# Rotary embedding on one core: four batches to a tile, the first tile in one piece, and tables of 32 partitions spread by TensorE

## The chip, the cores and the metric

The kernel runs on one core of a Trainium2 chip. The metric is the device time in microseconds (us), the median of several executions. A separate profiled execution leaves a trace; its span runs from the first instruction to the end of the last transfer, and all places in time ("at 92 us") count from its start.

## What is computed

`x` holds 16 batches of 512 rows of 1024 floats; a row is 16 heads of 64 values, and each head is split into two halves of 32. `cos` and `sin` have one row of 32 values for each of the 512 positions. In and out are 33.5 MB each, all in 32-bit floats.

```
x1, x2 = x[..., :half_dim], x[..., half_dim:]          # x as (16, 512, 16 heads, 64)
cos, sin = cos[None, :, None, :], sin[None, :, None, :]
out = concatenate([x1 * cos - x2 * sin, x1 * sin + x2 * cos], axis=-1)
```

## The kernel before, in words

**Rows and tiles.** A *row* in the kernel (index `u`, 0 to 63) is one row of x on each of 128 partitions: 128 rows of 4 KB, 0.5 MB in all. Rows come in tiles that are loaded by one DMA and stored by one DMA. The first two and last two tiles (L40) are one batch each, 4 rows, 2 MB, 16 KB in a piece per partition. The six between are two batches each, 8 rows, 4 MB, 32 KB per partition, with the two batches on alternate partitions (L108 to L111). In a tile of one batch, a partition holds 4 neighbouring positions, in a tile of two batches 8, so the two kinds need tables laid out differently.

**The ring.** `x_sb` holds 40 of the 64 rows. The loads of rows 0 to 39 are issued at once on ACT's queue, the tables' two loads right behind the first (L167 to L175). The loads of rows 40 to 63 reuse places: ACT issues them in the middle of its work, after rows 17, 25 and 33, and each waits first until the store of the rows that lay there before has landed (L193 to L196). The wait after row 33 is for the store of rows 16 to 23, and two loads follow it.

**One row.** There are two products and a sum. DVE multiplies the row by cos into PSUM (`mul`, L302; three such buffers). POOL multiplies the row with its halves swapped by a table of -sin and +sin into `t2_sb` (L263; eight buffers), mostly two rows in an instruction. In a tile of 8, row 3's swapped product is DVE's (`V2`, L295). The sum is DVE's (`comb`, L313, written over the row in `x_sb`) or, for rows 1, 3 and 5 of eight (`PE2`, L51, not in the first and last four rows), TensorE's: it adds the product to the PSUM buffer with a matmul by the identity (L225), and ACT copies the result to `x_sb` (L192). DVE's product for row u waits until the buffer of row u - 3 is free, so it can wait for ACT's copy.

**Stores.** SP issues the store of a tile once its last row is summed (L162).

**Tables.** cos and sin are loaded as 128 partitions of 4 positions (512 B each). The first tile's tables come straight from there: DVE copies cos (L273), ACT makes -sin and +sin (L183, L184). The tables for tiles of two batches are spread by TensorE: ACT makes `pick` from an identity (L178), two matmuls (L209) put positions of two partitions side by side in PSUM, and ACT makes -sin and +sin again (L187, L188). DVE copies the row it needs for row 3 (L280, L281). POOL waits for the first table at row 0 and the second at row 8 (L252 to L255).

Of the kernel before, what the change touches and what calls it, by code (L numbers as in the profile page):

```python
# [6 lines left out]
def bass_split_heads_rope_kernel(  # L7
# [16 lines left out]
    batch, seq, dim = x.shape  # L24
    H = int(num_heads)
# [4 lines left out]
    R2 = 2 * R1  # L30
    assert R1 * P == seq and R1 == 4 and batch % 2 == 0

# [6 lines left out]

    singles = (0, 1, batch - 2, batch - 1)  # L40
    tiles = [(b, R1 if b in singles else R2) for b in range(batch) if b in singles or b % 2 == 0]
    NT = len(tiles)
    RING = 5 * R2

    rows = [(t, r) for t, (_, n) in enumerate(tiles) for r in range(n)]
    NU = len(rows)
    EARLY = (NU - RING) // R2


    V_ROW = 3  # L50
    PE2 = [R1 <= u < NU - R1 and u % R2 in (1, 3, 5) for u in range(NU)]  # L51
    V2 = [tiles[t][1] == R2 and r == V_ROW for t, r in rows]

# [18 lines left out]
    with ExitStack() as stack:  # L72
        x_sb = stack.enter_context(nc.sbuf_tensor([P, RING, H, 2, HALF], fp32))
        t2_sb = stack.enter_context(nc.sbuf_tensor([P, NT2, H, 2, HALF], fp32))
        stage = stack.enter_context(nc.sbuf_tensor([P, 2, R1 * HALF], fp32))
        s1_sb = stack.enter_context(nc.sbuf_tensor([P, R1, 2, HALF], fp32))
        s2_sb = stack.enter_context(nc.sbuf_tensor([P, R2, 2, HALF], fp32))
        ident = stack.enter_context(nc.sbuf_tensor([P, P], fp32))
        pick = stack.enter_context(nc.sbuf_tensor([P, 2, P // 2, 2], fp32))
        zero = stack.enter_context(nc.sbuf_tensor([P, BANK], bf16))  # L80
        tab_ps = stack.enter_context(nc.psum_tensor([P, BANK], fp32))
        pair_ps = stack.enter_context(nc.psum_tensor([P, 2, 2, R1, HALF], fp32))
        t1_ps = stack.enter_context(nc.psum_tensor([P, NT1, H * HD], fp32))
# [17 lines left out]

        c1_ps = tab_ps[:, 0:R1 * HALF].rearrange("p (r d) -> p r d", d=HALF)
        v_ps = tab_ps[:, R1 * HALF:R1 * HALF + HD].rearrange("p (t d) -> p t d", d=HALF)

        def c_of(t, r):
            return c1_ps[:, r, :] if tiles[t][1] == R1 else pair_ps[:, r // R1, 0, r % R1, :]

        x1 = x.rearrange("b (s r) d -> b s (r d)", r=R1)  # L108
        o1 = out.rearrange("b (s r) h d -> b s (r h d)", r=R1)
        x2 = x.rearrange("b (s r) d -> s b (r d)", r=R2)  # L110
        o2 = out.rearrange("b (s r) h d -> s b (r h d)", r=R2)  # L111
        xs = x_sb[:].rearrange("p n h t d -> p n (h t d)")

        def in_dram(single, pairs, t):
            b, n = tiles[t]
            return single[b] if n == R1 else pairs[:, b:b + 2, :]

        def in_sbuf(t):
            b, n = tiles[t]
            k = b * R1 % RING  # L120
            return x_sb[:, k:k + n].rearrange("p n h t d -> p (n h t d)")
# [5 lines left out]
        def swapped(k):  # L127
            return x_sb[:, k, :, ::-1, :]
# [20 lines left out]
        def stores_of(k):  # L149

            return sum(b * R1 // R2 == k for b, _ in tiles)

        def load(eng, t):
            eng.dma_start(in_sbuf(t), in_dram(x1, x2, t)).then_inc(sem_in[t], 16)  # L154

        def on_sync(sp):
            for u in range(NU):
                t, r, k = where(u)
                if r == tiles[t][1] - 1:
                    wait_added(sp, u)  # L160
                    k = u // R2
                    sp.dma_start(in_dram(o1, o2, t), in_sbuf(t)).then_inc(sem_out[k] if k < EARLY else sem_rest, 16)  # L162
            sp.wait_ge(sem_rest, 16 * sum(stores_of(k) for k in range(EARLY, NU // R2)))

        def on_scalar(ae):
            later = {}
            for t, (b, n) in enumerate(tiles):  # L167
                if b * R1 + n <= RING:
                    load(ae, t)
                else:  # L170

                    later.setdefault((b * R1 - RING) // R2 * R2 + R2 - 1 + LAG, []).append(t)
# [5 lines left out]
            ae.activation(  # L178
                pick[:], ident[:].rearrange("q (s k) -> q k s", k=2)[:, :, :, None].broadcast_to([P, 2, P // 2, 2]), COPY
            ).then_inc(sem_g, 1)  # L180
            ae.wait_ge(sem_sin, 16)
            sv = stage[:, 1, :].rearrange("s (r d) -> s r d", d=HALF)
            ae.activation(s1_sb[:, :, 0, :], sv, COPY, scale=-1.0)  # L183
            ae.activation(s1_sb[:, :, 1, :], sv, COPY).then_inc(sem_s, 1)  # L184
            ae.wait_ge(sem_t, 2)
            s2 = s2_sb[:].rearrange("p (k r) t d -> p k r t d", r=R1)
            ae.activation(s2[:, :, :, 0, :], pair_ps[:, :, 1, :, :], COPY, scale=-1.0)  # L187
            ae.activation(s2[:, :, :, 1, :], pair_ps[:, :, 1, :, :], COPY).then_inc(sem_s, 1)  # L188
            for u in range(NU):
                if PE2[u]:  # L190
                    ae.wait_ge(sem_e, n_pe[u])
                    ae.activation(xs[:, u % RING, :], t1_ps[:, u % NT1, :], COPY).then_inc(sem_a, 1)  # L192
                for t in later.get(u, ()):  # L193
                    k = (tiles[t][0] * R1 - RING) // R2
                    ae.wait_ge(sem_out[k], 16 * stores_of(k))
                    load(ae, t)  # L196

        def on_tensor(pe):
# [6 lines left out]
            pe.wait_ge(sem_g, 1)  # L205
            pe.wait_ge(sem_cos, 16)
            pe.wait_ge(sem_sin, 16)
            for k in range(2):
                pe.matmul(  # L209
                    pair_ps[:, k].rearrange("p c r d -> p (c r d)"),  # L210
                    pick[:, k].rearrange("q s b -> q (s b)"),
                    stage[:].rearrange("q c f -> q (c f)"),
                    start=True,
                    stop=True,
                ).then_inc(sem_t, 1)
# [19 lines left out]
        def on_gpsimd(pl):  # L235
# [11 lines left out]
            for u in range(NU):  # L247
                if V2[u] or (G2[u] and u % 2 == 1):
                    continue
                t, r, k = where(u)  # L250
                n = 2 if G2[u] else 1
                if (t, r) == (0, 0):  # L252
                    pl.wait_ge(sem_s, 1)
                if (t, r) == (2, 0):
                    pl.wait_ge(sem_s, 2)  # L255
                if r == 0:
                    pl.wait_ge(sem_in[t], 16)
                if n == 2 and u + 1 >= NT2:
# [3 lines left out]
                table = (s1_sb if tiles[t][1] == R1 else s2_sb)[:, r:r + n]  # L262
                pl.tensor_tensor(  # L263
                    t2_sb[:, u % NT2:u % NT2 + n],
                    x_sb[:, k:k + n, :, ::-1, :],
                    table[:, :, None, :, :].broadcast_to([P, n, H, 2, HALF]),
                    mult,
                ).then_inc(sem_p, 1)

        def on_vector(ve):  # L270
            ve.memset(zero[:], 0.0).then_inc(sem_z, 1)  # L271
            ve.wait_ge(sem_cos, 16)
            ve.tensor_copy(c1_ps, stage[:, 0, :].rearrange("s (r d) -> s r d", d=HALF)).then_inc(sem_c, 1)  # L273
            ve.wait_ge(sem_c, 1)
            ve.wait_ge(sem_w, NT1 * EH)

            def pair_tables():
                ve.wait_ge(sem_s, 2)
                row = pair_ps[:, V_ROW // R1, 1, V_ROW % R1, :]
                ve.tensor_scalar_mul(v_ps[:, 0, :], row, -1.0).then_inc(sem_c, 1)  # L280
                ve.tensor_copy(v_ps[:, 1, :], row).then_inc(sem_c, 1)  # L281

            first_v = V2.index(True)

            def mul(u):
                t, r, k = where(u)
                if r == 0:
                    ve.wait_ge(sem_in[t], 16)
                if (t, r) == (2, 0):
                    pair_tables()  # L290
                if u == first_v:
                    ve.wait_ge(sem_c, 3)
                if V2[u]:
                    wait_t2_free(ve, u)
                    ve.tensor_tensor(t2_sb[:, u % NT2, :, :, :], swapped(k), over_heads(v_ps), mult)  # L295
                if u >= NT1:
# [7 lines left out]
                    x_sb[:, k, :, :, :].rearrange("p h t d -> p (h t) d"),  # L304
                    c_of(t, r)[:, None, :].broadcast_to([P, 2 * H, HALF]),
                    mult,
# [57 lines left out]
```

## Time and profile before

| | us |
|---|---|
| runs: median (lowest to highest) | 161.18 (161.13 to 161.49) |
| the profiled execution: span | 159.6 |
| what a run's time has around that span (median less span) | 1.6 |
| busy: DVE / POOL / PE / ACT | 129.6 / 131.7 / 64.4 / 24.3 |
| one POOL product of two rows (x23) / of one row (x12) | 4.53 / 2.36 |
| one DVE product / sum | 1.22 / 1.22 |
| one ACT copy of a row | 1.02 |
| moved by DMA | 67.25 MB, 421 GB/s over the span |
| first load lands / last load lands / last store issued | 8.5 / 140.25 / 151.9 |

An operation's own time includes a little overlap with the next: in a row of DVE operations one starts every 1.13 us, in a row of POOL products every 4.5 us (two rows) or 2.28 us (one row). The trace has for each DMA its issue, its size and the time to its landing; the queue q10 is ACT's (loads), q1 SP's (stores).

### The profile page before, as it was taken

To read this page: it belongs to the slowest core of one execution; us is meant where nothing else is said; L and a number is where in the kernel's file an instruction comes from. 1 tells how busy PE (TensorE), PEld (TensorE's weight loads), DVE (VectorE), ACT (ScalarE), POOL (GpSimd) and SP (SyncE) were. 2 spreads that over 40 slices of the span, in tenths; PEclk is the share of its full clock that TensorE was granted. 3 is DMA by queue.
4 is the path that set the end of the run, shared out by engine and by line. 5 is a ranking of instruction groups with operands and counts; after the bars stand their busy time and mean duration, and the time that the engine had idled before them with its cause. 6 is when DMAs were issued, how large, how long until landed. Compare 5 with 4: busy or idle time off the path is not lost.

```text
span 159.6 us, 499 instructions
## 1 busy us (share of the span) xinstructions
PE 64.4 (40%) x94; PEld 22.2 (14%) x94; DVE 129.6 (81%) x117; ACT 24.3 (15%) x27; POOL 131.7 (82%) x41
## 2 busy tenths in 40 slices
PE   6050017076408870789067400575058506900000
PEld 1020011021102220222021100211021102300000
DVE  0069947999999989998999629999999999556900
ACT  0420002004300250023102040023202310220000
POOL 1069999999999999999999798992999999089400
PEclk9999999759985589557759985589957995585555
DMA  5999999999999999999999999999999999999997
GB/s 144 396 466 472 394 411 431 448 476 402 394 448 406 495 419 402 476 435 402 443 435 435 394 476 435 402 460 394 427 456 448 443 394 423 472 419 435 386 456 300
DMA packets 3169, 67.25 MB, mean 421 GB/s; under 512 B 352, under 2 KB 608, under 8 KB 608
## 3 DMA queue, kind: packets, MB, share of 16 engines
q10 hardware_dynamic: 1728, 33.69, 49.8%
q1 hardware_dynamic: 1440, 33.56, 48.9%
q14 instruction: 1, 0.01, 0.0%
HBM read 33.69 MB, written 33.55 MB: 421 GB/s over the span
## 4 chain that ended last, share of the span: by engine, by line
DMA 61%; DVE 17%; POOL 5%; PE 5%; issue 4%; ACTq 1%; ACT 1%; DVEq 0%; POOLq 0%; SPq 0%
DMA x_sb<-in_x_dram 43%; DMA out_dram<-x_sb 18%; DVE t_ps L302 8%; DVE x_sb L313 7%; POOL t_sb L263 5%; PE t_ps L225 5%; DVE t_sb L295 2%; ACT x_sb L192 1%; ACTq L154 1%; ACTq L175 1%; DVE tab_ps L280 0%; DVEq L312 0%; DVE tab_ps L281 0%; DVEq L299 0%; POOLq L259 0%
## 5 line engine op out<-in xcount | busy, mean ns | idle before, releaser
L263 POOL TENSOR_TENSOR t_sb<-x_sb,s_sb 128x2048 f32<-128x2048 f32 (+1 forms) x35 | 131.0, 3784 | 17.1 <-DMA x_sb<-in_x_dram 8.3
L225 PE MATMUL t_ps<-t_sb,ident 128*128 128x512 f32 x84 | 59.6, 857 | 69.1 <-DVE t_ps L302 56.7
L302 DVE TENSOR_TENSOR t_ps<-x_sb,pair_ps 128x1024 f32<-128x1024 f32 x48 | 57.5, 1221 | 5.2 <-ACT x_sb L192 5.2
L313 DVE TENSOR_TENSOR x_sb<-t_ps,t_sb 128x1024 f32<-128x1024 f32 x43 | 52.2, 1216 | 5.9 <-POOL t_sb L263 5.9
L192 ACT ACTIVATE x_sb<-t_ps 128x1024 f32<-128x1024 f32 x21 | 21.4, 1024 | 107.6 <-PE t_ps L225 99.9
L225 PEld LDWEIGHTS t_ps<-t_sb,ident 128*128 128x128 f32 x84 | 20.3, 267 | 108.2 <-DVE t_ps L302 78.7
L302 DVE TENSOR_TENSOR t_ps<-x_sb,tab_ps 128x1024 f32<-128x1024 f32 x16 | 19.2, 1222 | 2.6 <-DMA x_sb<-in_x_dram 2.5
L295 DVE TENSOR_TENSOR t_sb<-x_sb,tab_ps 128x1024 f32<-128x1024 f32 x6 | 7.3, 1209 | 0.0
L273 DVE COPY tab_ps<-stage 128x128 f32<-128x128 f32 x1 | 0.3, 296 | 7.6 <-DMA stage<-in_cos_dram 7.6
L209 PE MATMUL pair_ps<-stage,pick 128*128 128x256 f32 x4 | 2.0, 667 | 5.1 <-DMA stage<-in_sin_dram 5.1
L202 PE MATMUL t_ps<-zero 128*128 128x512 bf16 x6 | 2.7, 629 | 1.3 <-DVE zero L271 1.3
L178 ACT ACT_TABLE_LOAD x1 | 1.3, 1283 | 5.5 <-issue 5.5
L209 PEld LDWEIGHTS pair_ps<-stage,pick 128*128 128x128 f32 x4 | 1.2, 324 | 6.1 <-issue 6.0
L202 PEld LDWEIGHTS t_ps<-zero 128*128 128x128 bf16 x6 | 0.7, 136 | 2.4 <-DVE zero L271 1.2
L271 DVE MEMSET zero<- 128x256 uint32 x1 | 0.3, 272 | 0.9 <-PEq L346 0.9
L187 ACT ACTIVATE s_sb<-pair_ps 128x256 f32<-128x256 f32 x1 | 0.4, 384 | 1.7 <-PE pair_ps L209 1.7
L183 ACT ACTIVATE s_sb<-stage 128x128 f32<-128x128 f32 x1 | 0.3, 310 | 1.8 <-DMA stage<-in_sin_dram 1.8
L236 POOL MEMSET ident<- 128x128 f32 x1 | 0.2, 205 | 0.3 <-POOLq L346 0.3
L178 ACT ACTIVATE pick<-ident 128x256 f32<-128x256 f32 x1 | 0.4, 416 | 0.0
L188 ACT ACTIVATE s_sb<-pair_ps 128x256 f32<-128x256 f32 x1 | 0.4, 377 | 0.0
L238 POOL TENSOR_SCALAR_AFFINE_SELECT ident<-ident 128x128 f32<-128x128 f32 x1 | 0.3, 295 | 0.1
L346 POOL MEMSET const-float32-0.0<- 128x1 f32 x1 | 0.1, 99 | 0.3 <-issue 0.3
(6 smaller groups left out, 1.0 us busy)
## 6 DMA issues: line engine op xcount, KB each, us to landing
x_sb<-in_x_dram ACTq DMA_DIRECT2D x6, 4096.0 KB, 38.7
out_dram<-x_sb SPq DMA_DIRECT2D x6, 4096.0 KB, 25.3
x_sb<-in_x_dram ACTq DMA_DIRECT2D x4, 2048.0 KB, 22.7
out_dram<-x_sb SPq DMA_DIRECT2D x4, 2048.0 KB, 16.1
stage<-in_cos_dram ACTq DMA_DIRECT2D x1, 64.0 KB, 7.5
stage<-in_sin_dram ACTq DMA_DIRECT2D x1, 64.0 KB, 7.2
```

The lines of the kernel that those rows point to most:

```text
L154: eng.dma_start(in_sbuf(t), in_dram(x1, x2, t)).then_inc(sem_in[t], 16)
L175: ae.dma_start(stage[:, i, :], table.rearrange("(s r) d -> s (r d)", r=R1)).then_inc(sem, 16)
L178: ae.activation(pick[:], ident[:].rearrange("q (s k) -> q k s", k=2)[:, :, :, None].broadcast_to([P, 2, P // 2, 2]), COPY).then_inc(sem_g, 1)
L187: ae.activation(s2[:, :, :, 0, :], pair_ps[:, :, 1, :, :], COPY, scale=-1.0)
L192: ae.activation(xs[:, u % RING, :], t1_ps[:, u % NT1, :], COPY).then_inc(sem_a, 1)
L202: pe.matmul(t1_ps[:, k, b * BANK:(b + 1) * BANK], zero[:, 0:P], zero[:], start=True, stop=True).then_inc(sem_w, 1)
L209: pe.matmul(pair_ps[:, k].rearrange("p c r d -> p (c r d)"), pick[:, k].rearrange("q s b -> q (s b)"), stage[:].rearrange("q c f -> q (c f)"),
L225: ins = pe.matmul(t1_ps[:, u % NT1, b * BANK:(b + 1) * BANK], ident[:], t2[:, b * BANK:(b + 1) * BANK], start=False, stop=True, skip_group ...
L263: pl.tensor_tensor(t2_sb[:, u % NT2:u % NT2 + n], x_sb[:, k:k + n, :, ::-1, :], table[:, :, None, :, :].broadcast_to([P, n, H, 2, HALF]), ...
L295: ve.tensor_tensor(t2_sb[:, u % NT2, :, :, :], swapped(k), over_heads(v_ps), mult)
L302: ve.tensor_tensor(t1_ps[:, u % NT1, :].rearrange("p (h d) -> p h d", d=HALF), x_sb[:, k, :, :, :].rearrange("p h t d -> p (h t) d"), c_of ...
L313: ve.tensor_tensor(xs[:, k, :], t1_ps[:, u % NT1, :], t2_sb[:, u % NT2, :, :, :].rearrange("p h t d -> p (h t d)"), add,).then_inc(sem_v, 1)
```

## The change

A tile now comes from a run of four batches (2048 rows): a partition holds 16 neighbouring positions of one batch, and 32 partitions make a batch. Each run of 16 rows is two tiles of 8 rows, the lower and the upper half of each partition's positions; only the very last tile stays cut in two of 4. So there are seven tiles of 4 MB and two of 2 MB. The pieces of a 4 MB tile are 32 KB each, 64 KB apart. The first tile is 4 MB, loaded and stored whole. All tiles share one layout of the tables: 16 positions on each of 32 partitions, loaded as 32 partitions of 2 KB, spread to all four batches by one matmul each for cos and sin (`pick` is an identity of 32, repeated four times). ACT makes -sin and +sin from the second matmul's result; DVE reads cos directly from PSUM, and for rows 3 and 11 makes -sin in the place next to sin. The direct tables for the first tile go. Five loads are issued up front instead of six.

```diff
+    R4 = 4 * R1
...
-    singles = (0, 1, batch - 2, batch - 1)
-    tiles = [(b, R1 if b in singles else R2) for b in range(batch) if b in singles or b % 2 == 0]
+    runs = batch // 4
+    tiles = []
+    for c in range(runs):
+        for r0 in range(0, R4, R2):
+            if (c, r0) == (runs - 1, R4 - R2):
+                tiles += [(c, r0, R1), (c, r0 + R1, R1)]
+            else:
+                tiles.append((c, r0, R2))
...
-    V_ROW = 3
+    V_ROWS = (3, 11)
     PE2 = [R1 <= u < NU - R1 and u % R2 in (1, 3, 5) for u in range(NU)]
-    V2 = [tiles[t][1] == R2 and r == V_ROW for t, r in rows]
+    V2 = [tiles[t][2] == R2 and r == V_ROWS[0] for t, r in rows]
...
+        xr = x.rearrange("(c b) (s r) d -> c (b s) r d", b=4, r=R4)
+        outr = out.rearrange("(c b) (s r) h d -> c (b s) r (h d)", b=4, r=R4)
...
+        def in_dram(view, t):
+            c, r0, n = tiles[t]
+            return view[c][:, r0:r0 + n, :].rearrange("p r d -> p (r d)")
...
-                        ae.dma_start(stage[:, i, :], table.rearrange("(s r) d -> s (r d)", r=R1)).then_inc(sem, 16)
+                        ae.dma_start(stage[:, i, :], table.rearrange("(s r) d -> s (r d)", r=R4)).then_inc(sem, 16)
...
+            ae.activation(pick[:], ident[0:P // 4, None, 0:P // 4].broadcast_to([P // 4, 4, P // 4]), COPY).then_inc(sem_g, 1)
             ae.wait_ge(sem_t, 2)
...
+            ae.activation(s_sb[:, :, 0, :], sin_ps, COPY, scale=-1.0)
+            ae.activation(s_sb[:, :, 1, :], sin_ps, COPY).then_inc(sem_s, 1)
...
+            for i, (table_ps, sem) in enumerate(((cos_ps, sem_cos), (sin_ps, sem_sin))):
+                pe.wait_ge(sem, 16)
                 pe.matmul(
+                    table_ps.rearrange("p r d -> p (r d)"),
+                    pick[:].rearrange("q b s -> q (b s)"),
+                    stage[:, i, :],
...
-                if (t, r) == (0, 0):
+                if u == 0:
                     pl.wait_ge(sem_s, 1)
-                if (t, r) == (2, 0):
-                    pl.wait_ge(sem_s, 2)
...
-            ve.wait_ge(sem_cos, 16)
-            ve.tensor_copy(c1_ps, stage[:, 0, :].rearrange("s (r d) -> s r d", d=HALF)).then_inc(sem_c, 1)
-            ve.wait_ge(sem_c, 1)
             ve.wait_ge(sem_w, NT1 * EH)
+            ve.wait_ge(sem_t, 1)
+
+            def v_table():
+                ve.wait_ge(sem_s, 1)
+                for r in V_ROWS:
+                    ve.tensor_scalar_mul(sin_ps[:, r - 1, :], sin_ps[:, r, :], -1.0).then_inc(sem_c, 1)
...
-                if (t, r) == (2, 0):
-                    pair_tables()
+                if u == first_v - 1:
+                    v_table()
```

More of the change, by code (lines that the diff above doesn't have):

```diff
@@ L30, in bass_split_heads_rope_kernel @@
     R2 = 2 * R1
-    assert R1 * P == seq and R1 == 4 and batch % 2 == 0
+    R4 = 4 * R1
+    assert R1 * P == seq and R1 == 4 and batch % 4 == 0
     fp32 = mybir.dt.float32
@@ L37, in bass_split_heads_rope_kernel @@
     COPY = mybir.ActivationFunctionType.Copy
-    singles = (0, 1, batch - 2, batch - 1)
-    tiles = [(b, R1 if b in singles else R2) for b in range(batch) if b in singles or b % 2 == 0]
+    runs = batch // 4
[6 more added lines that the diff above has]
+                tiles.append((c, r0, R2))
     NT = len(tiles)
     RING = 5 * R2
-    rows = [(t, r) for t, (_, n) in enumerate(tiles) for r in range(n)]
+    rows = [(t, r) for t, (_, _, n) in enumerate(tiles) for r in range(n)]
     NU = len(rows)
     EARLY = (NU - RING) // R2
-    V_ROW = 3
+    V_ROWS = (3, 11)
     PE2 = [R1 <= u < NU - R1 and u % R2 in (1, 3, 5) for u in range(NU)]
-    V2 = [tiles[t][1] == R2 and r == V_ROW for t, r in rows]
+    V2 = [tiles[t][2] == R2 and r == V_ROWS[0] for t, r in rows]
     def count(flags):
@@ L74, in bass_split_heads_rope_kernel @@
         t2_sb = stack.enter_context(nc.sbuf_tensor([P, NT2, H, 2, HALF], fp32))
-        stage = stack.enter_context(nc.sbuf_tensor([P, 2, R1 * HALF], fp32))
-        s1_sb = stack.enter_context(nc.sbuf_tensor([P, R1, 2, HALF], fp32))
-        s2_sb = stack.enter_context(nc.sbuf_tensor([P, R2, 2, HALF], fp32))
+        stage = stack.enter_context(nc.sbuf_tensor([P // 4, 2, R4 * HALF], fp32))
+        s_sb = stack.enter_context(nc.sbuf_tensor([P, R4, 2, HALF], fp32))
         ident = stack.enter_context(nc.sbuf_tensor([P, P], fp32))
-        pick = stack.enter_context(nc.sbuf_tensor([P, 2, P // 2, 2], fp32))
+        pick = stack.enter_context(nc.sbuf_tensor([P // 4, 4, P // 4], fp32))
         zero = stack.enter_context(nc.sbuf_tensor([P, BANK], bf16))
-        tab_ps = stack.enter_context(nc.psum_tensor([P, BANK], fp32))
-        pair_ps = stack.enter_context(nc.psum_tensor([P, 2, 2, R1, HALF], fp32))
+        cos_bank = stack.enter_context(nc.psum_tensor([P, BANK], fp32))
+        sin_bank = stack.enter_context(nc.psum_tensor([P, BANK], fp32))
         t1_ps = stack.enter_context(nc.psum_tensor([P, NT1, H * HD], fp32))
@@ L100, in bass_split_heads_rope_kernel, with table_row @@
         sem_a = stack.enter_context(nc.semaphore("act"))
[L102 to L111, printed above, removed]
+        cos_ps = cos_bank[:].rearrange("p (r d) -> p r d", d=HALF)
+        sin_ps = sin_bank[:].rearrange("p (r d) -> p r d", d=HALF)
+        def table_row(u):
+            return u % R4
+        xr = x.rearrange("(c b) (s r) d -> c (b s) r d", b=4, r=R4)
+        outr = out.rearrange("(c b) (s r) h d -> c (b s) r (h d)", b=4, r=R4)
         xs = x_sb[:].rearrange("p n h t d -> p n (h t d)")
-        def in_dram(single, pairs, t):
-            b, n = tiles[t]
-            return single[b] if n == R1 else pairs[:, b:b + 2, :]
+        def in_dram(view, t):
+            c, r0, n = tiles[t]
+            return view[c][:, r0:r0 + n, :].rearrange("p r d -> p (r d)")
         def in_sbuf(t):
-            b, n = tiles[t]
-            k = b * R1 % RING
+            c, r0, n = tiles[t]
+            k = (c * R4 + r0) % RING
             return x_sb[:, k:k + n].rearrange("p n h t d -> p (n h t d)")
@@ L149, in stores_of @@
         def stores_of(k):
-            return sum(b * R1 // R2 == k for b, _ in tiles)
+            return sum((c * R4 + r0) // R2 == k for c, r0, _ in tiles)
         def load(eng, t):
-            eng.dma_start(in_sbuf(t), in_dram(x1, x2, t)).then_inc(sem_in[t], 16)
+            eng.dma_start(in_sbuf(t), in_dram(xr, t)).then_inc(sem_in[t], 16)
         def on_sync(sp):
@@ L158, in on_sync @@
                 t, r, k = where(u)
-                if r == tiles[t][1] - 1:
+                if r == tiles[t][2] - 1:
                     wait_added(sp, u)
                     k = u // R2
-                    sp.dma_start(in_dram(o1, o2, t), in_sbuf(t)).then_inc(sem_out[k] if k < EARLY else sem_rest, 16)
+                    sp.dma_start(in_dram(outr, t), in_sbuf(t)).then_inc(sem_out[k] if k < EARLY else sem_rest, 16)
             sp.wait_ge(sem_rest, 16 * sum(stores_of(k) for k in range(EARLY, NU // R2)))
@@ L166, in on_scalar @@
             later = {}
-            for t, (b, n) in enumerate(tiles):
-                if b * R1 + n <= RING:
+            for t, (c, r0, n) in enumerate(tiles):
+                if c * R4 + r0 + n <= RING:
                     load(ae, t)
                 else:
-                    later.setdefault((b * R1 - RING) // R2 * R2 + R2 - 1 + LAG, []).append(t)
+                    later.setdefault((c * R4 + r0 - RING) // R2 * R2 + R2 - 1 + LAG, []).append(t)
                 if t == 0:
                     for i, (table, sem) in enumerate(((cos, sem_cos), (sin, sem_sin))):
-                        ae.dma_start(stage[:, i, :], table.rearrange("(s r) d -> s (r d)", r=R1)).then_inc(sem, 16)
+                        ae.dma_start(stage[:, i, :], table.rearrange("(s r) d -> s (r d)", r=R4)).then_inc(sem, 16)
             ae.wait_ge(sem_i, 2)
[L178 to L184, printed above, removed]
+            ae.activation(pick[:], ident[0:P // 4, None, 0:P // 4].broadcast_to([P // 4, 4, P // 4]), COPY).then_inc(sem_g, 1)
             ae.wait_ge(sem_t, 2)
-            s2 = s2_sb[:].rearrange("p (k r) t d -> p k r t d", r=R1)
-            ae.activation(s2[:, :, :, 0, :], pair_ps[:, :, 1, :, :], COPY, scale=-1.0)
-            ae.activation(s2[:, :, :, 1, :], pair_ps[:, :, 1, :, :], COPY).then_inc(sem_s, 1)
+            ae.activation(s_sb[:, :, 0, :], sin_ps, COPY, scale=-1.0)
+            ae.activation(s_sb[:, :, 1, :], sin_ps, COPY).then_inc(sem_s, 1)
             for u in range(NU):
@@ L193, in on_scalar @@
                 for t in later.get(u, ()):
-                    k = (tiles[t][0] * R1 - RING) // R2
+                    k = (tiles[t][0] * R4 + tiles[t][1] - RING) // R2
                     ae.wait_ge(sem_out[k], 16 * stores_of(k))
@@ L205, in on_tensor @@
             pe.wait_ge(sem_g, 1)
-            pe.wait_ge(sem_cos, 16)
-            pe.wait_ge(sem_sin, 16)
-            for k in range(2):
+            for i, (table_ps, sem) in enumerate(((cos_ps, sem_cos), (sin_ps, sem_sin))):
+                pe.wait_ge(sem, 16)
                 pe.matmul(
-                    pair_ps[:, k].rearrange("p c r d -> p (c r d)"),
-                    pick[:, k].rearrange("q s b -> q (s b)"),
-                    stage[:].rearrange("q c f -> q (c f)"),
+                    table_ps.rearrange("p r d -> p (r d)"),
+                    pick[:].rearrange("q b s -> q (b s)"),
+                    stage[:, i, :],
                     start=True,
@@ L261, in on_gpsimd @@
                     wait_t2_free(pl, u)
-                table = (s1_sb if tiles[t][1] == R1 else s2_sb)[:, r:r + n]
+                table = s_sb[:, table_row(u):table_row(u) + n]
                 pl.tensor_tensor(
@@ L271, in on_vector @@
             ve.memset(zero[:], 0.0).then_inc(sem_z, 1)
-            ve.wait_ge(sem_cos, 16)
-            ve.tensor_copy(c1_ps, stage[:, 0, :].rearrange("s (r d) -> s r d", d=HALF)).then_inc(sem_c, 1)
-            ve.wait_ge(sem_c, 1)
             ve.wait_ge(sem_w, NT1 * EH)
[L277 to L281, printed above, removed]
+            ve.wait_ge(sem_t, 1)
[3 more added lines that the diff above has]
+                    ve.tensor_scalar_mul(sin_ps[:, r - 1, :], sin_ps[:, r, :], -1.0).then_inc(sem_c, 1)
             first_v = V2.index(True)
@@ L288, in mul @@
                     ve.wait_ge(sem_in[t], 16)
-                if (t, r) == (2, 0):
-                    pair_tables()
+                if u == first_v - 1:
+                    v_table()
                 if u == first_v:
-                    ve.wait_ge(sem_c, 3)
+                    ve.wait_ge(sem_c, 2)
                 if V2[u]:
                     wait_t2_free(ve, u)
-                    ve.tensor_tensor(t2_sb[:, u % NT2, :, :, :], swapped(k), over_heads(v_ps), mult)
+                    ve.tensor_tensor(t2_sb[:, u % NT2, :, :, :], swapped(k), over_heads(sin_ps[:, table_row(u) - 1:table_row(u) + 1, :]), mult)
                 if u >= NT1:
@@ L304, in mul @@
                     x_sb[:, k, :, :, :].rearrange("p h t d -> p (h t) d"),
-                    c_of(t, r)[:, None, :].broadcast_to([P, 2 * H, HALF]),
+                    cos_ps[:, table_row(u), :][:, None, :].broadcast_to([P, 2 * H, HALF]),
                     mult,
```

## The prediction

> **What bounds the kernel now.** I read the page's second part first, because it says at once whether any engine or the DMA is full.
>
> ```profile
> span 159.6 us, 499 instructions
> ...
> DMA  5999999999999999999999999999999999999997
> GB/s 144 396 466 472 394 411 431 448 476 402 394 448 406 495 419 402 476 435 402 443 435 435 394 476 435 402 460 394 427 456 448 443 394 423 472 419 435 386 456 300
> ```
>
> The 16 DMA engines are full from about 3 us to the end, at about 427 GB/s between 56 and 136 us. DVE and POOL are at 81% and 82%. So 67.25 MB have to be drained, and nothing shortens the run that doesn't drain them faster. But the drain is only as good as its supply: it must never run empty. The profiled execution spans 159.6 us; the median of the runs is 161.18, so I add 1.6 to a span.
>
> The second view is the DMA queues in two short windows, first 45 to 49 us, where the store moves 16 KB pieces, then 60 to 65 us, where it moves 32 KB pieces (queue q10 is the loads, q1 the stores; columns are packets, MB, share).
>
> ```profile
> q10 hardware_dynamic: 33, 1.08, 62.5%
> q1 hardware_dynamic: 32, 0.52, 30.6%
> ```
> ```profile
> q1 hardware_dynamic: 32, 1.05, 48.7%
> q10 hardware_dynamic: 32, 1.05, 48.5%
> ```
>
> With both queues full they take turns packet by packet. A store in 16 KB pieces gets a third of the rate, one in 32 KB pieces gets half. That sets how long a store takes. The DMA issues in four windows give each store's time to landing; the timeline gives their issues at 20.19, 31.64, 47.46 and 63.81.
>
> ```profile
> out_dram<-x_sb SPq DMA_DIRECT2D x1, 2048.0 KB, 18.2
> ```
> ```profile
> out_dram<-x_sb SPq DMA_DIRECT2D x1, 2048.0 KB, 21.3
> ```
> ```profile
> out_dram<-x_sb SPq DMA_DIRECT2D x1, 4096.0 KB, 25.2
> ```
> ```profile
> out_dram<-x_sb SPq DMA_DIRECT2D x1, 4096.0 KB, 28.2
> ```
>
> So the landings are 38.4, 52.9, 72.7 and 92.0. Behind another store, a 2 MB one takes 52.9 - 38.4 = 14.5 and a 4 MB one 92.0 - 72.7 = 19.35. The first took 18.2, so a store that starts on an empty queue costs 18.2 - 14.5 = 3.7 more.
>
> The third view is the timeline where compute stalls: after 92 us, and after 140 us.
>
> ```profile
> 92.04 1.53 ACTq L154 DMA_DIRECT2D x_sb<-in_x_dram  x2
> 93.61 1.94 ACT L192 ACTIVATE x_sb<-t_ps 128x1024 f32<-128x1024 f32 x2 [7.78 <-issue]
> 94.67 2.36 DVE L302 TENSOR_TENSOR t_ps<-x_sb,pair_ps 128x1024 f32<-128x1024 f32 x2 [4.41 <-ACT x_sb L192]
> ...
> 140.28 2.36 DVE L302 TENSOR_TENSOR t_ps<-x_sb,tab_ps 128x1024 f32<-128x1024 f32 x2 [2.53 <-DMA x_sb<-in_x_dram]
> ...
> 144.92 1.22 DVE L313 TENSOR_TENSOR x_sb<-t_ps,t_sb 128x1024 f32<-128x1024 f32 x1 [2.29 <-POOL t_sb L263]
> ```
>
> ACT, after row 33, waits in its own queue (L195) for the store of rows 16 to 23, which lands at 92.02, before it issues the last loads. Its copies (L192) stand behind that wait, and DVE waits 4.41 us for them. From there DVE runs without a gap until 137.7, then waits 2.53 for the last load (landing at 140.25) and 2.29 for POOL, which waited for the same load. So the chain "third store group lands, ACT is freed, DVE works off the rest, last store" has 2.53 + 2.29 = 4.82 us of slack today, and the drain decides.
>
> **The start, today.** The timeline again:
>
> ```profile
> 8.78 0.30 DVE L273 COPY tab_ps<-stage 128x128 f32<-128x128 f32 x1 [7.58 <-DMA stage<-in_cos_dram]
> 9.07 2.05 PE L209 MATMUL pair_ps<-stage,pick 128*128 128x256 f32 x4 [5.08 <-DMA stage<-in_sin_dram]
> 9.55 22.70 POOL L263 TENSOR_TENSOR t_sb<-x_sb,s_sb 128x1024 f32<-128x1024 f32 x7 [8.18 <-ACT s_sb L184]
> 27.87 1.23 DVE L313 TENSOR_TENSOR x_sb<-t_ps,t_sb 128x1024 f32<-128x1024 f32 x1 [0.98 <-POOL t_sb L263]
> ```
>
> The first load (2 MB) lands at 0.81 + 7.7 = 8.5, cos at 8.7, sin at 8.9. The small tables need no TensorE: POOL starts at 9.55, row 7 is added at 31.6.
>
> **The change, part by part.**
>
> *First tile whole.* Two loads of 2 MB become one of 4 MB ahead of the tables. The second load lands at 13.8 today, with the same 4.3 MB ahead of it, so the first tile lands at 13.4, cos at 13.5, sin at 13.7: 4.8 later. Nothing covers this, since POOL and DVE have nothing else to do.
>
> *Tables by TensorE.* DVE's copy (0.30) and ACT's two (0.31 and 0.29) go. In their place stand two matmuls of 128x512. Today four records of 256 columns took 2.05, one table's worth of 512 columns thus 1.0; a pair of 512-column fp32 matmuls at L225 took from 1.98 (at 85.79) to 3.39 (at 23.44, after a pause), and by columns 2.05 becomes 4.1. PE has paused here too, so I take 3.4 for both, bounds 2.0 and 4.1. cos is there at 13.7 + 1.7 = 15.4, sin at 17.1. DVE starts its first products at 15.4 (9.11 today), which doesn't matter: its first sum waits for POOL. ACT then makes two copies of 128x512: 0.38 for 256 columns (L187), 1.02 for 1024 (L192), by interpolation 0.6 each, 1.1 together. POOL starts at 17.1 + 1.1 + 0.2 = 18.4, bounds 16.6 and 20.1. Behind POOL's wait for the table stand all its products. The smaller pick (0.42 today) lies long before, at 6.8.
>
> *Row 3 to DVE.* The first tile has 8 rows now, so row 3's swapped product goes from POOL (2.28 in a row of singles) to DVE (1.13 in a row). POOL does rows 0 to 7 in 18.2 - 2.3 = 15.9 us, to 34.3 (27.7 today). DVE gets one operation and two table rows (0.1 each, as L280 and L281 today). DVE's first sum begins 2.46 after POOL (12.01 today), at 20.9; the table rows (0.2) and 12 steps of 1.13 later row 6's sum begins, at 34.7. So both arrive together. Today row 7's sum ends 3.7 after row 6's begins (27.87 to 31.57), 3.5 without the table rows between. So rows 0 to 7 are done at 38.3.
>
> *One store of 4 MB.* The first store leaves at 38.3 instead of 20.19 and 31.64. It runs in 32 KB pieces at half the rate: 3.7 + 19.35 = 23.05, landing at 61.4. Today the same rows were out at 52.9. The next two leave 15.9 and 31.8 later (54, 70; eight rows take 14 DVE steps of 1.13), both behind a store still running: they land at 80.7 and 100.1. The loads keep the other half: the five up front need 9.7 a tile alone (13.8 to 23.5 today), so when the store's bytes begin, some 1.4 after its issue, 1.24 tiles are left, gone at 63.7, and the next load is issued at 61.4. That is just in time, so the half share holds. SP issues 9 stores for 10, ACT 9 loads for 10; an issue is 0.3 to 0.6 on a queue that waits anyway.
>
> *The sum.* ACT reaches its wait after row 33 about 21 us after row 23's sum, at 92 to 93, and is held to 100.1 (92.02 today). All loads come in time now: the last lands at about 132, needed at 147. So from the landing on, today's 159.6 - 92.0 = 67.6 less its slack of 4.82 remains: 62.8. It ends with the same 7.7 us for the last 2 MB. The span is 100.1 + 62.8 = 162.9, and the time **164.5 us**. In steps: the third group lands 8.1 later, 4.8 is slack, 3.3 remain. The drain, which would end at 159.4 to 159.6, would stand idle some 3 us late in the run, waiting for DVE. POOL isn't what holds: 34 products from 18.4 need 128.5 in all, to 147, plus what it waits for DVE.
>
> Unknown costs: the table stretch is 1.8 less or 1.7 more (162.7 to 166.2). The rate of a 64 KB step between partitions is not in the trace. Steps of 16 KB (loads, 4 to 20 us) gave 431 GB/s, steps of 32 KB between pairs two batches apart 427; the lowest and highest stretch of 8 us gave 406 and 468. I take 427.
>
> **Rivals.**
>
> 1. *The drain hides it all.* If the store of rows 16 to 23 lands by 96.8, the slack of 4.8 swallows the shift and the span stays 159.6, 161.2 us in all. For it: the DMA is full in every slice. Against it: 3.3 us would have to come from somewhere, and the table bounds give 1.8. If the loads run dry at 63.7, stores get the whole rate for a moment, worth perhaps 1 us. Chance 0.07.
> 2. *Faster.* The drain decides and is shorter. Place: loads run alone to 38 us rather than 20, and the 256 table packets of 512 B (322 packets moved only 355 GB/s from 7.4 to 8.6, a loss of 0.2 us) become 64. If loads alone ran at 468, as from 8 to 16, 18 us more of them would save 18 x 41 / 427 = 1.7. Price: 0.2 to 1.7 less, 159.5 to 161.0. It decides only if the third group lands by about 96. Against it: 4 to 20 us, loads alone, averages 431. Chance 0.08.
> 3. *A slower drain.* All nine tiles now step 64 KB between partitions. At the lowest stretch's 406 GB/s the drain alone takes 67.25 / 0.406 = 166 us behind 3, some 170 in all; half that loss gives 167. Nothing in the rows asks for it. Chance 0.07. The Trainium skill (DMA: Bandwidth & Descriptors, section Latency and other measured facts) says that large power-of-two distances between partitions slow copies, 207 GB/s a direction at 512 KiB against 214 in full; it lists nothing at 64 KiB. By that 3% this would be about 166, and no run here shows it yet.
>
> **How the numbers follow.** The forecast (the ACT wait decides) has 0.78, 162.4 to 166.3. Range 161.6 to 167.0: it takes in the table bounds and half of the third rival, and leaves out the first two and that rival's far end. This kernel's measurement tells 0.2% (0.3 us) from no change. Faster 0.08, same 0.07, slower 0.85.
>
> **What would show it.** POOL's first product near 18.4 and the first store at 38.3; three stores landing near 61, 81 and 100; a gap on DVE released by ACT near 100, none released by a load near 140; a last store alone at about 155, with empty DMA slices shortly before it. POOL starting before 16 or a third landing before 97 would refute the sum; a mean rate off 427 while both queues are full would be the third rival.

## The result, and the profile after

The changed kernel takes 162.9 us (median of 5, 162.61 to 163.04), the kernel before 161.39 in the same comparison: a ratio of 1.0092, interval 1.0078 to 1.0107. It is slower, as forecast, by 1.5 us and not by the 3.3 of the forecast. The time of 162.9 lies within the range given, but the step is less than half of the one that was forecast. The profiled execution spans 161.5 us against 159.6. Times and ratios here and below are of executions in the fast state (three of hold's twelve and one of laterload's six were slower, 164.4 to 166.7 us, and are left out).

The second part of the page first, as before: the span, how full the DMA is, and what it moved.

```profile
span 161.5 us, 492 instructions
...
DMA  7999999999999999999899999999999999999997
GB/s 260 390 391 421 390 479 430 390 479 430 390 455 455 390 455 455 335 438 422 349 446 422 430 455 414 430 406 446 426 475 402 422 422 459 414 471 406 402 410 300
```

The DMA is as full as before, to the end. No slice is empty late in the run. But two slices are low, 335 and 349 GB/s, between 64 and 81 us. That is the first hint that the forecast's mechanism isn't the whole of it.

The timeline of the start, with the steps that the forecast priced (start, duration, engine and line):

```profile
13.83 2.04 PE L204 MATMUL cos_bank<-stage,pick 32*128 32x512 f32 x2 [9.84 <-DMA stage<-in_cos_dram]
...
15.67 1.91 PE L204 MATMUL sin_bank<-stage,pick 32*128 32x512 f32 x2
...
17.62 0.60 ACT L183 ACTIVATE s_sb<-sin_bank 128x512 f32<-128x512 f32 x1 [11.83 <-PE sin_bank L204]
...
18.78 27.17 POOL L256 TENSOR_TENSOR t_sb<-x_sb,s_sb 128x1024 f32<-128x1024 f32 x8 [17.42 <-ACT s_sb L184]
...
39.14 0.38 SPq L165 DMA_DIRECT2D out_dram<-x_sb  x1
```

POOL starts at 18.78 (18.4 forecast), the first store leaves at 39.14 (38.3). The stall around 100 us is there too:

```profile
99.32 0.85 ACTq L157 DMA_DIRECT2D x_sb<-in_x_dram  x2
100.22 1.94 ACT L188 ACTIVATE x_sb<-t_ps 128x1024 f32<-128x1024 f32 x2 [6.62 <-DMA out_dram<-x_sb]
101.27 2.36 DVE L292 TENSOR_TENSOR t_ps<-x_sb,cos_bank 128x1024 f32<-128x1024 f32 x2 [3.53 <-ACT x_sb L188]
```

The third store lands at 99.3 (forecast 100.1) and DVE is held 3.53 us by ACT. No wait for a load is left near 140. The last store leaves at 154.55 (155.2) and lands 6.9 us later (7.7). So far this reads as the forecast, 1.4 us shorter. But the DMA queues from 60 to 70 us (packets, MB, share) don't:

```profile
q1 hardware_dynamic: 121, 3.44, 84.5%
q10 hardware_dynamic: 33, 0.56, 14.1%
```

Stores take 84.5% of the engines' time, loads 14.1%; before the change it was 48.7% and 48.5% in this stretch. The last packets of the loads up front start at 59.7, the first of the next load (issued at 62.71) at 67.4: no load packet starts for 7.6 us, where about 2 is usual while the two queues take turns. This document calls that an empty load queue. And the drain is slower in this stretch. Here are the same stretches for the kernel before and then for the changed one; the last two columns are the DMA's share and GB/s:

```profile
60.00:80.00 20.00, 9.79 (x12) 3.38 (x12) 19.59 (x19) 3.08 (x3) 20.00 (x6) 0.68 1.01 437
80.00:100.00 20.00, 7.47 (x12) 2.53 (x12) 15.59 (x15) 2.96 (x3) 18.21 (x6) 0.76 0.99 428
```
```profile
60.00:80.00 20.00, 12.20 (x17) 4.07 (x16) 19.59 (x18) 4.09 (x4) 20.00 (x6) 0.68 1.01 403
80.00:100.00 20.00, 11.22 (x16) 3.77 (x16) 17.75 (x16) 3.07 (x3) 20.00 (x6) 0.74 0.99 426
```

The share is 1.01 in both, the rate 437 and 403. So the engines are as busy and move less: 34 GB/s over 20 us are 0.68 MB, 1.6 us of the drain. Up to 60 us both kernels have moved 24.8 MB, and from 80 to 140 us they move 25.9 and 25.8 MB. The packets show how. A packet of 32 KB takes 1.21 us in the median; between 62 and 82 us, 38 of 244 take 1.35 to 2.4, first stores around 66 us, then loads, mostly from 74 to 78. Adding up what all 16 and 32 KB packets after the start (from 4.5 us) take beyond the median of 1.213 us per 32 KB, and dividing by 16 engines, gives 0.7 us before the change and 2.4 after, 1.4 of it between 62 and 82 us, 0.5 near 13 us.

So there are two theories. **Wait theory**, the forecast's: the chain through ACT's wait decides. **Drain theory**: the drain decides, and it has become longer; its rival causes are the 64 KB step, the empty load queue, the whole load and the late store.

### The profile page after: what moved, and what is told of

It reads as the page before. It is cut to its first block, busy times and chain, and to the rows that moved or that the text cites. A ratio compares the mean times of both kernels' runs of the same rounds, so it can differ in the third digit from the quotient of the medians.

```text
span 161.5 us, 492 instructions
## 1 busy us (share of the span) xinstructions
PE 69.7 (43%) x94; PEld 23.2 (14%) x94; DVE 130.2 (81%) x117; ACT 24.1 (15%) x25; POOL 129.4 (80%) x40
## 4 chain that ended last, share of the span: by engine, by line
DVE 36%; DMA 25%; PE 14%; issue 14%; ACT 5%; POOL 1%; ACTq 1%; DVEq 0%; SPq 0%
DMA out_dram<-x_sb 17%; DVE t_ps L292 16%; DVE x_sb L303 16%; PE t_ps L220 12%; DMA stage<-in_cos_dram 8%; ACT x_sb L188 4%; DVE t_sb L285 4%; POOL t_sb L256 1%; PE cos_bank L204 1%; PE sin_bank L204 1%; ACTq L157 1%; ACT s_sb L183 0%; ACT s_sb L184 0%; DVE sin_bank L271 0%; DVEq L302 0%
## 5 line engine op out<-in xcount | busy, mean ns | idle before, releaser
L256 POOL TENSOR_TENSOR t_sb<-x_sb,s_sb 128x2048 f32<-128x2048 f32 (+1 forms) x34 | 128.7, 3817 | 19.5 <-ACT s_sb L184 17.4
L292 DVE TENSOR_TENSOR t_ps<-x_sb,cos_bank 128x1024 f32<-128x1024 f32 x64 | 76.7, 1221 | 20.5 <-PE cos_bank L204 14.8
L220 PE MATMUL t_ps<-t_sb,ident 128*128 128x512 f32 x84 | 63.2, 906 | 65.4 <-DVE t_ps L292 65.4
L220 PEld LDWEIGHTS t_ps<-t_sb,ident 128*128 128x128 f32 x84 | 21.4, 281 | 108.0 <-DVE t_ps L292 90.2
L285 DVE TENSOR_TENSOR t_sb<-x_sb,sin_bank 128x1024 f32<-128x1024 f32 x7 | 8.5, 1214 | 0.0
L204 PE MATMUL cos_bank<-stage,pick 32*128 32x512 f32 x2 | 2.0, 1122 | 9.8 <-DMA stage<-in_cos_dram 9.8
L183 ACT ACTIVATE s_sb<-sin_bank 128x512 f32<-128x512 f32 x1 | 0.6, 597 | 11.8 <-PE sin_bank L204 11.8
L204 PEld LDWEIGHTS cos_bank<-stage,pick 32*128 32x128 f32 x2 | 0.5, 306 | 10.7 <-issue 10.7
L204 PE MATMUL sin_bank<-stage,pick 32*128 32x512 f32 x2 | 1.9, 1056 | 0.0
L204 PEld LDWEIGHTS sin_bank<-stage,pick 32*128 32x128 f32 x2 | 0.7, 332 | 1.0 <-issue 1.0
L184 ACT ACTIVATE s_sb<-sin_bank 128x512 f32<-128x512 f32 x1 | 0.6, 592 | 0.0
```

The lines of the kernel that those rows point to most:

```text
L183: ae.activation(s_sb[:, :, 0, :], sin_ps, COPY, scale=-1.0)
L184: ae.activation(s_sb[:, :, 1, :], sin_ps, COPY).then_inc(sem_s, 1)
L204: pe.matmul(table_ps.rearrange("p r d -> p (r d)"), pick[:].rearrange("q b s -> q (b s)"), stage[:, i, :], start=True, stop=True,).then_in ...
L220: ins = pe.matmul(t1_ps[:, u % NT1, b * BANK:(b + 1) * BANK], ident[:], t2[:, b * BANK:(b + 1) * BANK], start=False, stop=True, skip_group ...
L256: pl.tensor_tensor(t2_sb[:, u % NT2:u % NT2 + n], x_sb[:, k:k + n, :, ::-1, :], table[:, :, None, :, :].broadcast_to([P, n, H, 2, HALF]), ...
L292: ve.tensor_tensor(t1_ps[:, u % NT1, :].rearrange("p (h d) -> p h d", d=HALF), x_sb[:, k, :, :, :].rearrange("p h t d -> p (h t) d"), cos_ ...
```

## The experiments

**The same kernel again**, for a second trace.

> The changed kernel unaltered, for a second trace of it. Both theories: 162.9 us. Wait theory (the chain from the third store's landing through ACT's wait to the last store sets the end): the landing near 99, DVE held 3 to 4 us by ACT behind it, the last store alone at about 154.5. Drain theory (the 16 DMA engines are full to the end, and single packets that take up to 2.4 us instead of 1.21 cost 1.9 us): the slow packets come back at the same three places, near 13, 66 and 77 us. If the places move, it is not the layout of the addresses alone that makes them.

162.5 us (ratio 1.0082, interval 1.0052 to 1.0112; the same two figures stand behind each time below). The slow packets come back at 12 to 13, 66 to 67 and 76 to 80 us, and a group at 42, where the first trace had few. 60 to 80 us: 405 GB/s. So it is no accident of one execution.

**ACT's last wait later** (late): does the wait decide?

```diff
-                    later.setdefault((c * R4 + r0 - RING) // R2 * R2 + R2 - 1 + LAG, []).append(t)
+                    later.setdefault((c * R4 + r0 - RING) // R2 * R2 + R2 - 1 + LAG + (4 if c * R4 + r0 >= NU - R2 else 0), []).append(t)
```

> Only the last wait of ACT moves, from behind row 33 to behind row 37, so two copies of ACT are no longer queued behind it. Wait theory: DVE's 3.5 us behind ACT near 100 us go, the last store leaves near 151 instead of 154.5, and the end falls back to the drain: 160.0 to 161.4 us. Drain theory: nothing that it needs has changed, 162.5 to 162.9 us.

163.3 us (1.0106, 1.0082 to 1.0130), no gain, and 0.4 above even the drain theory's range. The edit did what it should. ACT's copies of rows 35 and 37 now lie ahead of the wait:

```profile
95.56 1.02 ACT L188 ACTIVATE x_sb<-t_ps 128x1024 f32<-128x1024 f32 x1 [1.71 <-PE t_ps L220]
98.95 1.02 ACT L188 ACTIVATE x_sb<-t_ps 128x1024 f32<-128x1024 f32 x1 [2.37 <-PE t_ps L220]
100.04 0.88 ACTq L157 DMA_DIRECT2D x_sb<-in_x_dram  x2
```

DVE has no gap there, and the last store leaves 2.9 us earlier:

```profile
151.61 0.33 SPq L165 DMA_DIRECT2D out_dram<-x_sb  x1
```

But it lands 10.2 us after its issue instead of 6.9, because the stores ahead of it are still in the queue. The wait theory falls: taking 3 us off its chain gains nothing. In the changed kernel, too, the last store leaves (154.55) while the store ahead of it is still moving (it lands at 156.6); shorten the chain, and the drain still ends no earlier.

**The memory places** (oldaddr, oldlate, newaddr). Is it the 64 KB step? The changed kernel at the places of the kernel before, without and with the late wait, and the kernel before at the places of the changed one; orders and sizes stay.

```diff
...
-            c, r0, n = tiles[t]
-            return view[c][:, r0:r0 + n, :].rearrange("p r d -> p (r d)")
+            c, r0, n = tiles[t]
+            b = (c * R4 + r0) // R1
+            return view[0][b] if n == R1 else view[1][:, b:b + 2, :]
```

newaddr is the reverse, in the kernel before:

```diff
...
-            return single[b] if n == R1 else pairs[:, b:b + 2, :]
+            c, r0 = b // R1, b % R1 * R1
+            return single[c][:, r0:r0 + n, :].rearrange("p r d -> p (r d)")
```

> The changed kernel with every wait, order and size as it is, but its tiles are read from and written to the places in memory that the tiles of the kernel before have (two batches on alternate partitions, one batch for the last two). The rows then meet the tables of other positions, so the rotation is not that of the reference; its work and its time are the same in kind. Address theory (the 64 KB step between partitions makes the slow packets near 12, 42, 66 and 76 us, and the drain, which sets the end, is longer by them): the slow packets go, 161.0 to 161.7 us. Order theory (they come from the order of loads and stores: the first tile whole, the late first store): 162.4 to 162.9, with the slow packets in place.

> As oldaddr, and ACT's last wait behind row 37 as in late. Again the rows meet the tables of other positions. Address theory: if the drain is no longer slowed, the last store's leaving decides in oldaddr, and taking 3 us off that chain brings the time to the drain's, 160.7 to 161.3. Order theory: 162.4 to 163.3, as late.

> The kernel before with every wait, order and size as it is, but its tiles lie where those of the changed kernel lie, 64 KB apart between partitions. The rows meet the tables of other positions, so the rotation is not that of the reference. Address theory: slow packets appear, 161.9 to 162.9 us. Order theory: 161.1 to 161.5, as before.

newaddr: 161.29 us, ratio 0.9996 (0.9980 to 1.0011), no change. oldaddr: 163.9 (1.0130, 1.0097 to 1.0163), oldlate: 163.4 (1.0130, 1.0087 to 1.0173); both lie above what either theory expected, by 1.0 and 0.1 us, and why is open. The window from 60 to 80 us, newaddr and then oldaddr:

```profile
60.00:80.00 20.00, 10.00 (x12) 3.40 (x12) 19.44 (x19) 3.07 (x3) 20.00 (x6) 0.69 1.01 437
```
```profile
60.00:80.00 20.00, 12.25 (x17) 4.07 (x16) 19.59 (x19) 4.10 (x4) 20.00 (x6) 0.67 1.00 403
```

The slow stretch goes with the order, not with the places. The 64 KB step costs nothing that these runs can tell, and the forecast's third rival had the right effect and the wrong cause. The Trainium skill's warning (DMA: Bandwidth & Descriptors, Latency and other measured facts) of large power-of-two distances starts at 512 KiB; at 64 KB these runs show no loss.

**The first tile in two pieces again** (split), and then only its load or only its store.

```diff
-            if (c, r0) == (runs - 1, R4 - R2):
+            if (c, r0) in ((0, 0), (runs - 1, R4 - R2)):
```

> Only the first tile is cut in two of 2 MB again, as before the change; the layout of four batches and the spread tables stay. Wait theory: tables land near 8.9 us, POOL starts near 14, the first stores leave near 24 and 36, the third group lands at 92 to 95, and the end falls back to the drain: 161.0 to 161.6 us. Drain theory with the 64 KB step as its cause: the layout is still there, 162.4 to 162.9 us.

161.85 us (1.0025, 1.0013 to 1.0037), between the two ranges. POOL starts at 13.9, the first store leaves at 24.5, and 60 to 80 us run at 435 GB/s. Three quarters of the loss are gone, with the layout and the spread tables still there.

storesplit loads the first tile whole and stores its halves after rows 3 and 7:

```diff
...
-                if r == tiles[t][2] - 1:
+                if t == 0 and r % R1 == R1 - 1:
+                    wait_added(sp, u)
+                    half = x_sb[:, u + 1 - R1:u + 1].rearrange("p n h t d -> p (n h t d)")
+                    sp.dma_start(outr[0][:, u + 1 - R1:u + 1, :].rearrange("p r d -> p (r d)"), half).then_inc(sem_out[0], 16)
+                elif r == tiles[t][2] - 1:
```

> The changed kernel, whose first tile is loaded whole but stored in two halves of 2 MB (pieces of 16 KB), after rows 3 and 7. Restart theory: the halves get only a third of the DMA's turns, both have landed at 62 to 64 us, no earlier than the whole tile, the loads up front are through by 58 and their queue runs empty for longer, so 162.5 to 163.1 us, no gain. If the late first store as such were the cost, its leaving at 30.6 instead of 39 would bring it back to 161.6 to 162.0.

162.6 us (1.0076, 1.0060 to 1.0092), 405 GB/s, the load queue empty for 7.3 us. Storing half of the tile at 30.7 gains nothing here, where its other half leaves at 39.3.

loadsplit loads in halves and stores whole after row 7 (SP stores rows 0 to 7 with one DMA at u = 7, the rest as split):

> The kernel with the first tile loaded in two halves (split), but stored whole after row 7. Restart theory: the store leaves at 35.8 and lands near 59.5, the loads up front are through near 61, the next load's first packets come near 64, so the load queue runs empty for about 3 us: 162.0 to 162.6 us, between split (161.85) and the change (162.5 to 162.9). If only the time of the tables and of POOL's start matters: 161.8 to 162.0.

161.9 us (1.0029, 1.0015 to 1.0043), as split; the store leaves at 35.9.

**The same with the store 3.5 us later** (loadsplitwait). The edit is against loadsplit.

```diff
                         wait_added(sp, u)
+                        sp.wait_ge(sem_m, R2 + 3)
```

> The kernel with the first tile loaded in halves and stored whole (loadsplit), whose first store waits for three products of DVE more, so that it leaves near 39 as in the changed kernel instead of 35.8. Late-store theory (the loads up front run alone for too long, their queue is through at 60 and empty for 7 us, and under these conditions packets near 42, 66 and 76 us are slow): 162.4 to 163.0 us with slow packets there. Whole-load theory (the 4 MB load ahead of the tables, and with it the late start of POOL and DVE, is what costs): 161.7 to 162.1, as loadsplit.

162.75 us (1.0089, 1.0072 to 1.0106), the whole loss of the change. The first store, loadsplit and then loadsplitwait:

```profile
35.89 0.38 SPq L166 DMA_DIRECT2D out_dram<-x_sb  x1
```
```profile
39.43 0.37 SPq L167 DMA_DIRECT2D out_dram<-x_sb  x1
```

The window from 60 to 80 us, in the same order:

```profile
60.00:80.00 20.00, 9.78 (x17) 3.21 (x16) 18.36 (x17) 3.74 (x4) 20.00 (x6) 0.83 1.02 438
```
```profile
60.00:80.00 20.00, 12.08 (x17) 4.19 (x16) 18.32 (x17) 3.02 (x4) 20.00 (x6) 0.68 1.00 405
```

These two differ in one wait of SP. The first store leaves at 39.43 instead of 35.89, the next load is issued at 62.70 instead of 58.80, no load packet starts for 7.0 us instead of 3.2, and the drain loses 33 GB/s for 20 us. POOL starts at 14.0 in both (18.8 in the changed kernel), and the first load is cut in two in both. So the late store alone is enough for the loss, without the late start of compute and without the whole load.

**Is it the empty queue?** hold is split, with the load of rows 40 to 47 held back until row 23 is summed; laterload is the changed kernel with that load behind row 21.

The issue moves behind row 21 in both; hold has this as well:

```diff
+                    if k == 0:
+                        ae.wait_ge(sem_v, n_comb[3 * R2 - 1])
                     ae.wait_ge(sem_out[k], 16 * stores_of(k))
```

> The kernel with the first tile cut in two (split), and one thing more: the load of rows 40 to 47 is issued only when row 23 is summed, near 68 us, so that the load queue runs empty for some 6 us as it does in the changed kernel. Restart theory (the drain sets the end, and a queue that starts again after it ran empty costs the drain 1 to 1.4 us in packets that take up to 2.4 us instead of 1.21): slow packets near 72 and 80 us, and 162.7 to 163.2 us against 161.85 for split. If the step of 64 KB or the lateness of the first store is what costs: 161.7 to 162.0, as split.

161.6 us (1.0034, 1.0007 to 1.0061), as split. The load queue was empty from 64.9 to 71.4, for 6.4 us against 7.6 in the changed kernel (6.9 in again), and it cost nothing that shows:

```profile
60.00:80.00 20.00, 9.73 (x16) 3.21 (x16) 20.00 (x19) 4.87 (x5) 20.00 (x6) 0.83 0.99 428
```

> The changed kernel, whose load of rows 40 to 47 is issued after row 21 instead of row 17, some 5.6 us later, so that the load queue is empty for about 13 us instead of 7.6. If the slow packets near 66 and 76 us belong to that load's start, they move to about 72 and 82 us; if they belong to the stores or to the time, they stay. If the drain sets the end and an empty load queue as such costs nothing, as in hold: 162.5 to 163.0 us; if each us of emptiness costs, 163.5 us or more.

162.7 us (1.0085, 1.0065 to 1.0105), with 405 GB/s. The load is issued 3.4 us later (66.13), not 5.6, and the queue is empty for 10.6 us and not for 13; the slow packets move to 67 to 70 and 71 to 76 us. The first group follows the start of that load (first packets at 67.4, here at 70.3); the second comes earlier, as does the second store's landing (79.9, here 75.3). The last store leaves at 151.4 here, 3 us earlier than in the changed kernel, with the same time: a second time that the chain doesn't decide.

**The tables ahead of the first tile** (tabfirst, and splittab with the tile cut as well).

```diff
+                if t == 0:
+                    for i, (table, sem) in enumerate(((cos, sem_cos), (sin, sem_sin))):
+                        ae.dma_start(stage[:, i, :], table.rearrange("(s r) d -> s (r d)", r=R4)).then_inc(sem, 16)
                 if c * R4 + r0 + n <= RING:
                     load(ae, t)
...
-                if t == 0:
-                    for i, (table, sem) in enumerate(((cos, sem_cos), (sin, sem_sin))):
-                        ae.dma_start(stage[:, i, :], table.rearrange("(s r) d -> s (r d)", r=R4)).then_inc(sem, 16)
```

> Only the order of the first loads changes: the two table loads are issued ahead of the first tile, so the matmuls and ACT's copies lie beside the first tile's load. Wait theory: POOL starts near 13.8 instead of 18.8, the first store leaves near 34, everything behind it 4 to 5 us earlier, the last store near 150, and the drain decides: 160.5 to 161.5 us. Drain theory: 162.4 to 162.9 us.

> Both cures together: the first tile cut in two, and the tables loaded ahead of it. Restart theory: the load queue never runs empty, the tables' matmuls lie beside the first load, the first store leaves near 20 as before the change; 160.9 to 161.6 us, the drain with the smaller cost of the 64 table packets of 2 KB. If the step of 64 KB has a cost of its own, it stays at 161.8 to 162.2.

tabfirst: 162.3 us (1.0051, 1.0033 to 1.0069), between the two ranges. POOL starts at 14.2, the first store leaves at 34.6, 60 to 80 us run at 443 GB/s. But the first packets of x start at 2.8 us instead of 1.8, and 0.9 us go to slow packets between 36 and 39. splittab: 163.0 (1.0092, 1.0069 to 1.0115), a plain miss. Its profiled execution spans 160.9 us, with the same later start and 0.9 us of slow packets between 23 and 31, which is less than its runs lost; the rest is open.

**The late store in the kernel before** (beforehold).

```diff
-                    wait_added(sp, u)
+                    wait_added(sp, R2 - 1 if t == 0 else u)
```

> The kernel before the change, in its own layout, whose first store (rows 0 to 3) is held back until row 7 is summed, so that it leaves with the second near 31.6 us instead of 20.2. Nothing else is touched. Late-store theory in its wide form (a first store that leaves late lets the loads up front run through and makes packets slow when loads and stores meet again): the load queue is empty for some 10 us around 60 to 70, slow packets near its restart, 162.2 to 163.0 us. If it needs more than that (as hold suggests, whose empty queue cost nothing): 161.2 to 161.6.

163.4 us (1.0151, 1.0123 to 1.0180), 0.4 above the theory's range: holding back one store of 2 MB by 11 us costs the kernel before more than the whole change does. The way there isn't quite the same. The load queue is empty for 8.2 us, 60 to 80 us run at 424, not 403 GB/s, 0.5 us go to slow packets there, DVE waits up to 7.2 us for ACT, and the engines of the DMA end unevenly, with a last slice of 170 GB/s against 300.

## Why the prediction was right or wrong, point by point

- *First tile whole, tables by TensorE, row 3 to DVE.* Right. cos has landed at 13.7 as forecast, the two matmuls take 3.8 us (3.4 taken, bounds 2.0 and 4.1), ACT's copies 0.60 each as interpolated, POOL starts 0.4 and the first store leaves 0.8 later than forecast.
- *One store of 4 MB.* Its landing, 62.7, was forecast at 61.4. What failed is "That is just in time, so the half share holds". It counts 1.4 us from the store's issue to its first bytes, and nothing for the next load's. The first store's began 4.3 after its issue, and so the loads ran alone for longer and had landed at 62.5, not 63.7; the next load was issued 1.3 later than forecast, and its bytes began 4.7 after that. The trace before had the number already: its first store, issued at 20.19, moves its first packet at 23.87, the 3.7 that the same paragraph adds for a start on an empty queue. By 3.7 the next load's bytes would have come at 65.1, behind the end of the loads at 63.7. So the load queue was empty for 7.6 us, the second store had the DMA to itself in that time and took 17.2 us rather than 19.35. The third landed at 99.3, 0.8 ahead of the forecast: the late first landing (+1.3) and the fast second store (-2.1) nearly cancel, which is luck.
- *The sum.* From that landing to the last store's issue 55.2 us (55.1 forecast), so DVE's part was right. The last 2 MB took 6.9, not 7.7: the store ahead of it landed 2.1 us after its issue, 2.9 in the kernel before. So the span is 161.5 and not 162.9: 0.8 from the landing, 0.8 from the last store, 0.1 back in between. By the spans the change costs 1.9, by the medians 1.5.
- *"It would stand idle some 3 us late in the run, waiting for DVE."* This is the step that failed, and it was wrong in kind: the drain was kept at 159.4 to 159.6 by the rate of the kernel before (427 GB/s in the forecast; the trace has 429 from 56 to 136 us), and its own lengthening was put at nothing. The DMA's idle time between 3 us and the last four is 0.3 us (0.7 in again). late and laterload take 3 us off the chain and gain nothing. The chain that was forecast exists, with every wait in its place, but it isn't what sets the end; the drain does, 1.9 us longer than before, and 1.7 of that are slow packets. That the time rose, and into the range, is luck as far as the mechanism goes.
- *Rival 3, a slower drain.* It was given 0.07, and a slower drain is what happened, though in a few stretches only and by 1.9 us, not the 5 to 9 that it priced (166 to 170 us). Its sign was there ("a mean rate off 427 while both queues are full": 391 GB/s from 67 to 80 us), its cause, the 64 KB step, is excluded by newaddr.
- *Rival 2.* The small gain from the tables was put at 0.2 us and is smaller: the 256 packets of 512 B took 0.43 us of the 16 engines, the 64 of 2 KB 0.37. More than that is lost in slow packets just behind them, 0.5 us near 13.

What is shown: with everything else alike, the store of rows 0 to 7 leaving at 39.4 instead of 35.9 is enough for the whole loss (loadsplit against loadsplitwait). What separates the rates from 60 to 80 us over all runs is whether rows 0 to 7 have landed before the loads up front run out. Where they hadn't (they landed at 62 to 63 us, the loads' last packets started near 60), this stretch ran at 402 to 413 GB/s, in eight traces, and at 424 in beforehold; where they had (57.6 in split, 57.7 in hold, 58.5 in tabfirst, 58.8 in loadsplit, 55.9 in splittab, 53 before the change and in newaddr), at 428 to 444. That is an ordering of the runs, not a mechanism, and it orders that stretch and not the whole time: splittab runs at 444 GB/s there and still takes 163.0 us. Why packets then take up to twice their time stays open: an empty load queue alone doesn't do it (hold), nor the places in memory (newaddr, oldaddr), nor the whole load (loadsplitwait has it without).

## What to carry to other kernels

Where the DMA is full, price a change by what it does to the drain: count when each queue runs empty and starts again, and not only the chain of waits. A chain of waits that keeps pace with the drain looks like the cause in the trace; move it by a wait or two and see if the time follows. And a first store that leaves later is not free, even when the loads alone keep the DMA full meanwhile.

## What the runs showed of the hardware

- A DMA's first packet starts 1.0 us after its issue when the engines are idle (0.80 to 1.80), but 3.3 to 5.0 us after it, over all runs, when its own queue is empty and they are full of the other queue's packets (39.14 to 43.42 and 62.71 to 67.36 in the changed kernel), some three to four packets of 1.21. The Trainium skill (DMA: Bandwidth & Descriptors, Latency and other measured facts) gives some 600 ns to the first byte on this path. The idle start here agrees if it is counted from the end of the issuing instruction (0.80 + 0.37 to 1.80, 0.63 us); the starts beside a full queue take far longer.
- A packet of 32 KB that takes 1.21 us nearly everywhere takes up to 2.4 in certain stretches of the changed kernel, with the DMA's share of busy time at 1.01 from 60 to 80 us, as before the change. The share doesn't show such a loss, the GB/s beside it do.
- A matmul of 512 columns in 32-bit floats (two records in the trace) took 2.04 us after a pause of 9.8 us (13.83), 2.07 in splittab after 2.4 us, and 1.12 in tabfirst after 1.9 us.
